# First modulation in two blocks of 512 channels, and the last FFN product in two passes of two token tiles

## The chip, the cores and the metric

The kernel runs on one core of one Trainium2 chip. The metric is the device time of one execution in microseconds (us), the median of several runs. TensorE (PE) multiplies matrices, PEld is its weight load, VectorE is DVE, ScalarE is ACT, GpSimd is POOL, and SyncE (SP) issues most of the DMAs, in order.

## The reference

Two decoder layers on 1024 tokens of 1024 channels, in float32. What matters here:

```
c_act = silu(c)
for l in range(2):
    mod = c_act @ ada_w[l] + ada_b[l]               # 6 x 1024: shift_m, scale_m, gate_m, shift_f, ...
    h = rms_norm(x, g_pre_mix[l]) * (1 + scale_m) + shift_m
    proj = h @ w_in[l] + b_in[l]                    # q (512), k, v (256), u (512)
    ...                                             # attention, pooling mixer, output projection
    x = x + gate_m * rms_norm(mix, g_post_mix[l])
    h = rms_norm(x, g_pre_ffn[l]) * (1 + scale_f) + shift_f
    f = (silu(h @ w_gate[l]) * (h @ w_up[l])) @ w_down[l]
    x = x + gate_f * rms_norm(f, g_post_ffn[l])
```

## The kernel before

The tokens are taken in two halves of 512 (T), each in four tiles of 128 (NT). Every wide product is three float32r products of high and low parts (`mm3`, L228 to L233): `split` (L208) makes the high part on ACT (L210) and the low part on DVE (L211). Each operand is loaded, split, and used by TensorE. A scheduler of the framework lays out each engine's instructions ahead of time, by program order among what its own model of the time takes to be ready; on the chip each engine and each queue then runs in that fixed order, held by semaphores.

**The start.** `xs` are the four x tiles of the first half (L1173). `load_cols` (L280) fetches the small parameter rows over SP (L287) and transposes them. The shift and scale of layer 0's first norm are made in four blocks of 256 channels: `ada_first_load` (L295) fetches, for each of the two parts, a block of `ada_w[0]` (L300); `ada_first` (L303) multiplies its eight rows j with `c_act` and adds them up on DVE (L309, L311), 256 wide, for both parts; then TensorE adds over the partitions with a product against a column of ones (L317), and DVE adds the bias (L324, L329). `pre_norm_piece(0, k, ...)` transposes 128 channels of the normalised x (L461), applies scale and shift on ACT (L466) and splits the result into an `hT` tile. `q_pass` and `kv_pass` (L613, L587) then take channels k: 12 wide products (512 columns) and 12 narrow ones (256 columns) for each k. The loop at L1190 runs over the blocks: two pieces, the next block's modulation, two steps of `q_pass`, one of `kv_pass`. The second half's x is loaded (L1198) in the third round, into the `cfa` tiles that the modulation used, and normalised (L1199) for the later stages.

**The end.** The FFN's last product, `down` (L1077), is a Strassen scheme of seven products p1 to p7, of 11 blocks of 128 rows each; the blocks come in groups (L1060) of one and then two. For each group the left operand is loaded from DRAM (L1130) and split, the right operand is combined by `combine` (L1084) in place and split into `bh` and `ph` or `bl`, and four token tiles t accumulate in four PSUM banks. The last job is p4, with the right operand `combine(b21, b21, b12)`. When a tile is done, `e7` or `e4` adds it up (L1089) and `ended` takes the square sum (ACT, L410); for p4 of the last layer it calls `finish`: a chain of 12 small DVE instructions gives 1/rms (L418, L240 to L247), then per half row `scaled_add` multiplies by 1/rms and G, the gate times `g_post_ffn` (L510) and adds x (L511), and SP stores it (L544). The four tiles of the first half are finished in the same way (`between`, L1341) while p7 and p3 run.

Of the kernel before, what the change touches and what calls it, by code (L numbers as in the profile page):

```python
# [65 lines left out]
def hybrid_decoder_kernel(  # L66
# [146 lines left out]
    def weight(*srcs):  # L213
# [9 lines left out]
        return hi, lo  # L223

    ALLP = slice(0, P)
    tiles = [slice(t * P, (t + 1) * P) for t in range(NT)]
# [53 lines left out]
    def load_cols(l):  # L280
        rows = t_("rows", [P, P])[:NROW]
        r = 0
        for src, n in (
            (ada_b[l], 6 * KD), (g_pre_mix[l], KD), (g_pre_ffn[l], KD),
            (pool_scale[l], 4), (b_in[l, QKV:INW], 4),
        ):
            nc.sync.dma_start(rows[r : r + n, :], src.rearrange("(r p) -> r p", p=P))  # L287
            r += n
        bank = msc_bank()
        nc.tensor.transpose(bank[:, :NROW], rows, ident[:NROW, :NROW])  # L290
        cols = t_("cols", [P, NROW])
        nc.vector.tensor_copy(cols, bank[:, :NROW])
        return cols

    def ada_first_load(part, n0):  # L295
        w = t_("cfa" if n0 // (2 * P) % 2 else "cfb", [P, 4, T]).rearrange("p (j a) n -> p j (a n)", j=2).rearrange("p a (j n) -> p (a j) n", n=2 * P)
        src = ada_w[0].rearrange("(p j) n -> p j n", j=KD)
        c0 = part * D + n0
        for js in (slice(0, KD // 2), slice(KD // 2, KD)):
            nc.sync.dma_start(w[:, js, :], src[:, js, c0 : c0 + 2 * P])  # L300
        return w

    def ada_first(n0, ws, cols, ab):  # L303

        accs = [t_("ar", [P, 512])[:, : 2 * P] for _ in ws]
        for j in range(KD):
            for acc, w in zip(accs, ws):
                if j == 0:
                    nc.vector.tensor_scalar(acc, w[:, j, :], c_act[:, 0:1], None, op0=ALU.mult)  # L309
                else:  # L310
                    nc.vector.scalar_tensor_tensor(  # L311
                        acc, w[:, j, :], c_act[:, j : j + 1], acc, op0=ALU.mult, op1=ALU.add
                    )
        bank = msc_bank()
        for m in range(2):
            for i in range(2):
                nc.tensor.matmul(  # L317
                    bank[:, 2 * m + i : 2 * m + i + 1], accs[m][:, i * P : (i + 1) * P], ones[:, 0:1],
                    start=True, stop=True,
                )  # L320
        o = slice(n0 // P, n0 // P + 2)
        for m, part in enumerate((1, 0)):
            k0 = part * KD + n0 // P
            nc.vector.tensor_add(ab[:, m, o], bank[:, 2 * m : 2 * m + 2], cols[:, k0 : k0 + 2])  # L324
        ada_scale(ab, 0, o, cols)
# [115 lines left out]

    def after(ins, prev):
        tc.add_manual_dep(
            ins.ins, prev.ins.name,
            mybir.DependencyInfo(mybir.DependencyClass.NoSync, mybir.DependencyReason.DATA),
            reason="order on the same engine",
        )

    def pre_norm_raw(h, k, ab, prev=None, xs=None, hf=None):
# [82 lines left out]
    def finish(h, t, fn, ss, G, xt=None):  # L532

        rstd = inv_rms(ss[:, 2 * t : 2 * t + 2])
        rows = slice(t * P, (t + 1) * P)
        for i in range(2):
            cs = slice(i * 512, (i + 1) * 512)
            if xt is None:
                x_ = t_("ar", [P, 512])
                nc.sync.dma_start(x_, spill[h][rows, cs])  # L540
            else:
                x_ = xt[:, cs]
            scaled_add(fn[t][:, cs], rstd, G[:, cs], x_)
            nc.sync.dma_start(out[0, h * T + rows.start : h * T + rows.stop, cs], fn[t][:, cs])  # L544
# [42 lines left out]
    def kv_pass(l, hT, bq, qkvs, pairs=None):  # L587

        if pairs:
            dsts = [pairs[t // 2][:, t % 2 * 256 : t % 2 * 256 + 256] for t in range(NT)]  # L590
        else:
            dsts = [acc_bank()[:, :256] for _ in range(NT)]
        for k in range(KD):
            if k % 2 == 0:
                wh, wl = weight(
                    (ALLP, 2, w_in[l, k * P : (k + 2) * P, ATT:QKV].rearrange("(a p) n -> p a n", p=P))
                )
# [12 lines left out]
        for t in range(NT):  # L610
            nc.vector.tensor_add(qkvs[t][:, ATT:QKV], dsts[t], bq[:, ATT:QKV])

    def q_pass(l, hT, bq, qkvs):  # L613
        banks = [acc_bank() for _ in range(NT)]
        for k in range(KD):
            wh, wl = weight((ALLP, None, w_in[l, k * P : (k + 1) * P, 0:ATT]))
            hi, lo = hT[k]
# [458 lines left out]

    def down(l, wd, load, kept, fn, ended):  # L1077

# [35 lines left out]
        def e4(t, bank):  # L1114
# [5 lines left out]
            ("p3", "s4", b22.__getitem__, e3), ("p7", "s3", combine(b22, b12, b11), e7),  # L1120
            ("p4", "a22", combine(b21, b21, b12), e4),
        ]
        ahead = {"p1": B21, "p2": B12, "p5": B22}
        count = [0]
        for name, a, right, evict in jobs:
            banks = [acc_bank() for _ in range(NT)]
            for g, (p0, p1) in enumerate(DOWN_GROUPS):
                n = p1 - p0
                raw = part("raw", 1024).rearrange("p (i n) -> p i n", n=512)[:, :n, :]
                nc.sync.dma_start(raw, kept[a][:, p0:p1, :])  # L1130
                lh, ll = (part(tag, 1024).rearrange("p (i n) -> p i n", n=512)[:, :n, :] for tag in ("hi", "lo"))
                split(lh, ll, raw)
                src = right(g)
# [5 lines left out]
                if name in ahead:  # L1139
                    load(ahead[name], g)  # L1140
                whole = g in (1, len(DOWN_GROUPS) - 1)
                for some in [range(n)] if whole else [(i,) for i in range(n)]:
                    for t in range(NT):
                        for i in some:
                            mm3(
                                banks[t], lh[:, i, tiles[t]], ll[:, i, tiles[t]], *rights[i],
                                p0 + i == 0, p0 + i == NPAIR - 1,
                            )
                        if p1 == NPAIR and some[-1] == n - 1:
                            evict(t, banks[t])  # L1150
                            ended(name, t)
                for _ in range(n):
# [8 lines left out]
    def layer_rows(l, d):  # L1161
        bq = t_("bqkv", [P, QKV])
        nc.sync.dma_start(bq, b_in[l : l + 1, 0:QKV].to_broadcast([P, QKV]))
        sk = t_("sk", [P, NH])
        nc.sync.dma_start(sk, sinks[l : l + 1, :].to_broadcast([P, NH]))
        nc.vector.tensor_scalar(sk, sk, -1.0, None, op0=ALU.mult)
        d["bq"], d["nsink"] = bq, sk

    par = layer_cols(0)
# [5 lines left out]
    ada0 = [ada_first_load(part, 0) for part in (1, 0)]  # L1175
    normalise(0, xs, stats(xs), True)
    hts = {0: []}
    layer_rows(0, par)
    qkvs0 = [t_("qkv", [P, QKV]) for _ in range(NT)]
    queries0 = q_pass(0, hts[0], par["bq"], qkvs0)  # L1180
# [3 lines left out]
    def first_modulation(n0):  # L1184
        if n0 < D:
            ws = [ada_first_load(part, n0) for part in (1, 0)] if n0 else ada0
            ada_first(n0, ws, par["cols"], par["abm"])
# [18 lines left out]
    for l in range(DEPTH):  # L1206
# [112 lines left out]
        def ended(name, t):  # L1319
# [29 lines left out]
        run(  # L1349
            down(l, wd, load, kept, fn, ended), 7 * NPAIR,  # L1350
            (between(), 7 * NPAIR), (side, 3 * len(jobs) * ADA),
# [40 lines left out]
```

## Time and profile before

| | us |
|---|---|
| median of 3 runs (lowest, highest) | 1993.48 (1992.32, 1997.05) |
| the profiled execution, its own time | 1994.2 |
| span of that execution, first to last instruction | 1992.4 |
| PE busy in the span | 1888.4 (95%) |
| DVE busy | 1574.2 (79%) |
| ACT busy | 957.9 (48%) |

The profile shows one execution. 1.8 us of its own time lie outside its span. A busy TensorE is not the same as a TensorE at its peak, since matmuls overlap and run at one of two clocks.

### The profile page before, as it was taken

What the parts mean: (1) busy time and instruction counts of PE and PEld (TensorE: products, weight loads), DVE (VectorE), ACT (ScalarE), POOL (GpSimd) and SP (SyncE); (2) the same over time, 40 slices, a digit from 0 to 9 for tenths busy, and PEclk for the clock granted to TensorE, in tenths of its full rate; (3) what the DMA queues carried; (4) which work ended last, traced back from release to release, by engine and by line L of the source; (5) the groups of instructions that cost most, each with busy time, mean ns of one, the idle gap of its engine ahead of it and who ended that gap; (6) DMA issues with size and microseconds to landing.
All of it is one profiled execution on the core that took longest, in us unless ns stands there. A gap on an engine that the chain in (4) does not pass through costs nothing. (4 is left out here: it accounts for less than half of the span.)

```text
span 1992.4 us, 26087 instructions
## 1 busy us (share of the span) xinstructions
PE 1888.4 (95%) x8942; PEld 1555.2 (78%) x8942; DVE 1574.2 (79%) x2951; ACT 957.9 (48%) x1797; POOL 52.8 (3%) x100
## 2 busy tenths in 40 slices
PE   4889989999999999999999899899999999999996
PEld 4777778887888887778887777788788888878885
DVE  7788976669889886786878899656888888677686
ACT  4676785563222223444757658845522222234442
POOL 1000000011000000001000000000200000000000
PEclk9999999999999999999999899999999999999998
DMA  8645654465455456842556455446555654474351
GB/s 264 206 133 156 191 177 138 131 199 194 165 184 201 147 164 219 301 140 87 185 177 188 133 151 188 132 132 193 169 182 178 199 176 148 172 256 140 114 168 64
DMA packets 224644, 340.81 MB, mean 171 GB/s; under 512 B 16728, under 2 KB 121320, under 8 KB 224512
## 3 DMA queue, kind: packets, MB, share of 16 engines
q1 hardware_dynamic: 224480, 339.15, 51.6%
q8 instruction: 70, 1.15, 0.2%
q14 instruction: 62, 0.51, 0.1%
q0 software_dynamic: 32, 0.00, 0.0%
HBM read 264.10 MB, written 74.99 MB: 170 GB/s over the span
## 5 line engine op out<-in xcount | busy, mean ns | idle before, releaser
L210 ACT ACTIVATE hi<-raw 128x1024 fp32r<-128x1024 f32 (+1 forms) x382 | 331.6, 877 | 336.6 <-PE acc L232 219.3
L211 DVE TENSOR_TENSOR lo<-raw,hi 128x1024 fp32r<-128x1024 f32 (+1 forms) x382 | 380.5, 1001 | 81.8 <-ACT hi L210 81.4
L229 PE MATMUL acc<-t,hi 128*128 128x512 f32 x704 | 275.9, 392 | 5.3 <-ACT hi L210 5.3
L233 PE MATMUL acc<-t,lo 128*128 128x512 f32 x704 | 275.5, 392 | 3.8 <-DVE lo L211 3.8
L232 PE MATMUL acc<-t,hi 128*128 128x512 f32 x704 | 275.2, 391 | 0.0
L229 PE MATMUL acc<-bh,hi 128*128 128x512 f32 x616 | 239.1, 392 | 3.3 <-ACT bh L210 3.0
L233 PE MATMUL acc<-bh,lo 128*128 128x512 f32 x616 | 241.9, 393 | 0.0
L229 PE MATMUL acc<-hT,hi 128*128 128x512 f32 x480 | 192.2, 400 | 8.7 <-ACT hi L210 8.1
L1011 DVE TENSOR_TENSOR fn<-acc,fn 128x512 f32<-128x512 f32 x220 | 151.2, 687 | 52.6 <-PE acc L233 51.9
L232 PE MATMUL acc<-hT,hi 128*128 128x512 f32 x480 | 190.6, 397 | 0.0
L233 PE MATMUL acc<-hT,lo 128*128 128x512 f32 x480 | 188.0, 395 | 0.0
L229 PEld LDWEIGHTS acc<-t,hi 128*128 128x128 f32 x704 | 133.0, 189 | 34.4 <-ACT hi L210 7.1
L233 PEld LDWEIGHTS acc<-t,lo 128*128 128x128 f32 x704 | 133.0, 189 | 34.1 <-DVE lo L211 6.6
L232 PEld LDWEIGHTS acc<-t,hi 128*128 128x128 f32 x704 | 132.9, 189 | 27.7
L232 PE MATMUL acc<-ph,hi 128*128 128x512 f32 x376 | 150.1, 399 | 0.5 <-DVE ph L211 0.4
L229 PEld LDWEIGHTS acc<-bh,hi 128*128 128x128 f32 x616 | 115.7, 188 | 31.6 <-ACT bh L210 3.8
L233 PEld LDWEIGHTS acc<-bh,lo 128*128 128x128 f32 x616 | 116.7, 189 | 24.5
L210 ACT ACTIVATE bh<-two_b 128x512 fp32r<-128x512 f32 x120 | 74.8, 623 | 98.2 <-PE acc L233 91.0
L263 DVE SCALAR_TENSOR_TENSOR ada<-ar,c_act,ada 128x512 f32<-128x512 f32 x140 | 104.8, 748 | 15.3 <-DMA ar<-in_ada_w_dram 14.0
L229 PEld LDWEIGHTS acc<-hT,hi 128*128 128x128 f32 x480 | 91.6, 191 | 28.9 <-ACT hi L210 9.6
L949 ACT ACTIVATE fn<-fn 128x512 f32<-128x512 f32 x44 | 27.8, 633 | 166.3 <-DVE fn L1011 156.1
L233 PEld LDWEIGHTS acc<-hT,lo 128*128 128x128 f32 x480 | 91.2, 190 | 18.5
(271 smaller groups left out, 3794.7 us busy)
## 6 DMA issues: line engine op xcount, KB each, us to landing
ar<-in_ada_w_dram SPq DMA_DIRECT2D x160, 256.0 KB
raw<-in_w_gate_dram SPq DMA_DIRECT2D x44, 512.0 KB
raw<-in_w_up_dram SPq DMA_DIRECT2D x44, 512.0 KB
raw<-in_w_in_dram SPq DMA_DIRECT2D x80, 256.0 KB
raw<-keeps SPq DMA_DIRECT2D x40, 512.0 KB
keeps<-fn SPq DMA_DIRECT2D x66, 256.0 KB
raw<-keepa SPq DMA_DIRECT2D x30, 512.0 KB
two_b<-in_w_down_dram SPq DMA_DIRECT2D x30, 512.0 KB
```

The costliest lines, as they stand in the source:

```text
L210: nc.scalar.activation(hi, src, AF.Copy)
L211: nc.vector.tensor_sub(lo, src, hi.bitcast(F32))
L229: ins = nc.tensor.matmul(dst, lh, rh, start=first, stop=False)
L232: nc.tensor.matmul(dst, lh, rl, start=False, stop=False)
L233: return nc.tensor.matmul(dst, ll, rh, start=False, stop=last)
L263: nc.vector.scalar_tensor_tensor(acc, w, c_act[:, i : i + 1], acc, op0=ALU.mult, op1=ALU.add)
L949: nc.scalar.activation(g, g, AF.Silu)
L1011: nc.vector.tensor_add(halves_of(dst)[m], bank, halves_of(src)[m])
```

## The change

In `load_cols` and `layer_rows` the seven small loads of layer 0 go out on ACT's queue instead of SP's. The first modulation has two blocks of 512 channels. In the first block only the scale (part 1) is added up on DVE; the shift (part 0) is added up on TensorE: each 128x128 piece of `ada_w` is the stationary operand against a column of `c_act`, and all accumulate in one PSUM bank. Its loads go into the eight `hT` tiles, two rows j at a time, scale and shift by turns. The second block works as before, 512 wide, from the `cfa` and `cfb` tiles. The order is: first loads of q and kv weights, first block, four pieces, four steps of q and two of kv (the second block's loads are issued after the first pair), second block, the second half's x, then the same again. In `down` p4's right operand is split once, into tiles that took the place of `b12` and `b22`, and its `combine` moves into p7's loop. In the last layer p4 runs over all groups for tiles 0 and 1 and then once more for tiles 2 and 3, with left operands of 256 tokens. The products with G are taken out of the last `finish`: `ended` multiplies p7's and p4's halves by G, and `finish` needs one instruction per half row.

```diff
-            nc.sync.dma_start(rows[r : r + n, :], src.rearrange("(r p) -> r p", p=P))
+            (nc.sync if l else nc.scalar).dma_start(rows[r : r + n, :], src.rearrange("(r p) -> r p", p=P))
...
+    def ada_first_load(n0):
+        src = ada_w[0].rearrange("(p j) n -> p j n", j=KD)
+        ws = []
+        step = 4 if n0 else 2
+        for j in range(0, KD, step):
+            for part in (1, 0):
+                if n0:
+                    w = t_("cfb" if j else "cfa", [P, 4, T])
+                else:
+                    w = t_("hT", [P, 2 * T]).rearrange("p (j n) -> p j n", n=T)
+                c0 = part * D + n0
+                nc.sync.dma_start(w, src[:, j : j + step, c0 : c0 + T])
+                ws.append((part, j, w))
+        return ws
...
+        accs = {part: t_("ar", [P, 512]) for part in ((1,) if pe else (1, 0))}
+        for part, j0, w in ws:
+            for j in range(w.shape[1]):
+                c_ = c_act[:, j0 + j : j0 + j + 1]
+                if pe and part == 0:
+                    for i in range(4):
+                        ins = nc.tensor.matmul(
+                            bank[:, 4 + i : 5 + i], w[:, j, i * P : (i + 1) * P], c_,
+                            start=j0 + j == 0 and i == 0, stop=False,
+                        )
...
+                acc = accs[part]
+                if j0 + j == 0:
+                    nc.vector.tensor_scalar(acc, w[:, j, :], c_, None, op0=ALU.mult)
+                else:
+                    nc.vector.scalar_tensor_tensor(acc, w[:, j, :], c_, acc, op0=ALU.mult, op1=ALU.add)
...
             if xt is None:
...
+                scaled_add(fn[t][:, cs], rstd, G[:, cs], x_)
             else:
-                x_ = xt[:, cs]
-            scaled_add(fn[t][:, cs], rstd, G[:, cs], x_)
+                nc.vector.scalar_tensor_tensor(
+                    fn[t][:, cs], fn[t][:, cs], rstd, xt[:, cs], op0=ALU.mult, op1=ALU.add
+                )
...
+                if name == "p7":
+                    right4(g)
+                products(name, g, lh, ll, rights, banks, range(NT), evict)
...
+        name, a, _, evict = jobs[-1]
+        kept4 = []
+        for ts in ((0, 1), (2, 3)) if last else (range(NT),):
+            banks = {t: acc_bank() for t in ts}
+            for g, (p0, p1) in enumerate(DOWN_GROUPS):
+                n = p1 - p0
+                lh, ll = left_of(a, p0, p1, ts[0] * P, (ts[-1] + 1) * P)
+                if len(kept4) == g:
+                    tag = "one_" if p1 == 1 else "two_"
+                    pair = [t_(tag + b, [P, n, 512], F32R) for b in (B12, B22)]
+                    split(*pair, b21[g])
+                    kept4.append([[r[:, i, :] for r in pair] for i in range(n)])
+                products(name, g, lh, ll, kept4[g], banks, ts, evict)
...
-    first_modulation(0)
-    for n0 in range(0, D, 2 * P):
-        for k in (n0 // P, n0 // P + 1):
-            hts[0].append(pre_norm_piece(0, k, par["abm"], None, xs))
-        first_modulation(n0 + 2 * P)
-        for _ in range(2):
-            next(queries0)
-        next(keys0)
-        if n0 == D - 4 * P:
+    next(queries0)
+    next(keys0)
+    ada_first(0, ada0, par["cols"], par["abm"], True)
+    for half in range(2):
+        for k in range(half * HK, (half + 1) * HK):
+            hf = t_("uT", [P, HALO + T])[:, :T]
+            hts[0].append(pre_norm_piece(0, k, par["abm"], None, xs, None, hf))
+        for pair in range(HK // 2):
+            for _ in range(2):
+                next(queries0)
+            next(keys0)
+            if half == 0 and pair == 0:
+                ada1 = ada_first_load(D // 2)
+        if half == 0:
+            ada_first(D // 2, ada1, par["cols"], par["abm"], False)
             xs1 = load_residual(1)
...
             elif name == "p7":
                 square_sum(ss[1], t, 1, fn[1][t][:, 512:D])
+                if not nxt:
+                    nc.vector.tensor_mul(fn[1][t][:, 512:D], fn[1][t][:, 512:D], G[:, 512:D])
             elif name == "p4":
                 square_sum(ss[1], t, 0, fn[1][t][:, 0:512])
                 if not nxt:
+                    nc.vector.tensor_mul(fn[1][t][:, 0:512], fn[1][t][:, 0:512], G[:, 0:512])
                     finish(1, t, fn[1], ss[1], G, tail[t])
```

## Rows read from the trace of the kernel before

**Rows 1.** The page, busy us, share of the span, instructions of TensorE
```profile
PE 1888.4 (95%) x8942; PEld 1555.2 (78%) x8942; DVE 1574.2 (79%) x2951; ACT 957.9 (48%) x1797; POOL 52.8 (3%) x100
```

**Rows 2.** The timeline of TensorE, first 75 us: start, us, operation, idle before
```profile
22.63 1.01 PE L317 MATMUL msc<-ones_r,ar 128*128 128x1 f32 x4 [0.30 <-DVE ar L311]
29.98 0.99 PE L317 MATMUL msc<-ones_r,ar 128*128 128x1 f32 x4 [6.33 <-DVE ar L311]
30.83 1.20 PE L229 MATMUL acc<-hi,hT 128*128 128x512 f32 x2
...
32.25 0.63 PE L233 MATMUL acc<-hi,hT 128*128 128x512 f32 x1
...
42.44 1.04 PE L461 MATMUL msc<-ident,fn 128*128 128x128 f32 x8
...
54.92 0.50 PE L317 MATMUL msc<-ones_r,ar 128*128 128x1 f32 x4
55.28 0.48 PE L232 MATMUL acc<-lo,hT 128*128 128x512 f32 x1
...
74.61 0.40 PE L229 MATMUL acc<-hT,hi 128*128 128x512 f32 x1
```

**Rows 3.** Windows: stretch, length, busy PE, PEld, DVE, ACT, POOL, PEclk, DMA, GB/s
```profile
42.40:45.40 3.00, 2.51 (x23) 2.19 (x21) 2.57 (x8) 2.32 (x4) 0.00 (x0) 1.00 0.03 8
45.40:53.80 8.40, 8.40 (x51) 7.46 (x49) 8.37 (x22) 3.47 (x6) 0.00 (x0) 1.00 0.37 110
...
81.00:92.00 11.00, 9.36 (x57) 7.30 (x55) 9.22 (x31) 8.80 (x17) 0.00 (x0) 1.00 0.66 190
92.00:98.00 6.00, 4.18 (x18) 3.63 (x17) 4.17 (x14) 5.38 (x14) 0.00 (x0) 0.72 0.07 26
```

**Rows 4.** The timeline of TensorE, first and last product of p4
```profile
1944.46 0.39 PE L229 MATMUL acc<-bh,hi 128*128 128x512 f32 x1
...
1975.09 0.39 PE L233 MATMUL acc<-bh,lo 128*128 128x512 f32 x1
```

**Rows 5.** The timeline of DVE, the end
```profile
1971.39 0.69 DVE L1089 TENSOR_TENSOR sa<-acc,sa 128x512 f32<-128x512 f32 x1 [8.20 <-PE acc L233]
...
1976.65 1.41 DVE L510 SCALAR_TENSOR_TENSOR sa<-sa,rs,G 128x512 f32<-128x512 f32 x2
...
1988.14 1.28 DVE L511 TENSOR_TENSOR sb<-sb,hT 128x512 f32<-128x512 f32 x2
```

**Rows 6.** The timeline of DVE where p7 ends and p4 begins
```profile
1942.20 2.48 DVE L1089 TENSOR_TENSOR sa<-acc,sa 128x512 f32<-128x512 f32 x4
...
1947.58 1.23 DVE L211 TENSOR_TENSOR lo<-raw,hi 128x1024 fp32r<-128x1024 f32 x1
```

**Rows 7.** Instructions of the line of combine, from 1780 us on
```profile
L1084 DVE TENSOR_TENSOR two_b<-two_b,two_b x10: 1217/1220/1226, 1822.6 to 1845.1; 128x1024 f32<-128x1024 f32 x10
```

**Rows 8.** Instructions by line: DVE's sums of 256 and of 512 columns: ns min/median/max
```profile
L311 DVE SCALAR_TENSOR_TENSOR ar<-cfb,c_act,ar x28: 477/481/489, 12.3 to 44.0; 128x256 f32<-128x256 f32 x28
...
L263 DVE SCALAR_TENSOR_TENSOR ada<-ar,c_act,ada x140: 740/748/755, 64.9 to 1613.4; 128x512 f32<-128x512 f32 x140
```

**Rows 9.** The DMA view of the first 60 us, GB/s in 40 slices of 1.5 us
```profile
GB/s 0 128 336 292 366 332 287 329 352 343 275 253 331 377 358 376 380 382 350 348 313 104 277 274 299 307 368 180 25 0 11 40 315 193 1 117 407 415 306 388
```

**Rows 10.** Timelines of DVE, ACT and SP, the start
```profile
11.89 0.35 DVE L309 TENSOR_SCALAR ar<-cfb,c_act 128x256 f32<-128x256 f32 x1 [0.28 <-DMA cfb<-in_ada_w_dram]
...
5.06 0.63 ACT L410 ACTIVATE junk<-fn 128x512 bf16<-128x512 f32 x1 [2.49 <-DMA fn<-in_x_dram]
...
24.13 1.45 ACT L466 ACTIVATE raw<-msc,colp 128x512 f32<-128x512 f32 x2 [1.16 <-DVE colp L329]
25.47 1.14 ACT L210 ACTIVATE hT<-raw 128x512 fp32r<-128x512 f32 x2
...
3.60 0.53 SPq L287 DMA_DIRECT2D rows<-in_ada_b_dram  x1
```

**Rows 11.** The chain that ended last, in order of time, one piece
```profile
1921.03 3.63 DMA ar<-x
```

More of the change, by code (lines that the diff above doesn't have):

```diff
@@ L223, in weight, with after @@
         return hi, lo
+    def after(ins, prev):
+        tc.add_manual_dep(
+            ins.ins, prev.ins.name,
+            mybir.DependencyInfo(mybir.DependencyClass.NoSync, mybir.DependencyReason.DATA),
+            reason="order on the same engine",
+        )
     ALLP = slice(0, P)
@@ new lines, in ada_first_load, with ada_first @@
+        ws = []
[4 more added lines that the diff above has]
+                    w = t_("cfb" if j else "cfa", [P, 4, T])
+                else:
+                    w = t_("hT", [P, 2 * T]).rearrange("p (j n) -> p j n", n=T)
[3 more added lines that the diff above has]
+        return ws
+    def ada_first(n0, ws, cols, ab, pe):
+        bank = msc_bank()
+        accs = {part: t_("ar", [P, 512]) for part in ((1,) if pe else (1, 0))}
[8 more added lines that the diff above has]
+                        )
+                        if j0 + j == 0 and i == 0:
+                            opening = ins
+                        else:
+                            after(ins, opening)
+                    continue
+                acc = accs[part]
[3 more added lines that the diff above has]
+                    nc.vector.scalar_tensor_tensor(acc, w[:, j, :], c_, acc, op0=ALU.mult, op1=ALU.add)
+        for m, part in enumerate((1,) if pe else (1, 0)):
+            for i in range(4):
+                ins = nc.tensor.matmul(
+                    bank[:, 4 * m + i : 4 * m + i + 1], accs[part][:, i * P : (i + 1) * P], ones[:, 0:1],
+                    start=not pe, stop=not pe or i == 3,
+                )
+                if pe:
+                    after(ins, opening)
+        o = slice(n0 // P, n0 // P + 4)
@@ L440, in normalise @@
         normed[h] = dst
[L442 to L447, printed above, removed]
     def pre_norm_raw(h, k, ab, prev=None, xs=None, hf=None):
@@ L592, in kv_pass, with rows @@
             dsts = [acc_bank()[:, :256] for _ in range(NT)]
+        def rows(k):
+            return weight(
+                (ALLP, 2, w_in[l, k * P : (k + 2) * P, ATT:QKV].rearrange("(a p) n -> p a n", p=P))
+            )
+        ahead = None
+        if pairs:
+            ahead = rows(0)
+            yield
         for k in range(KD):
             if k % 2 == 0:
-                wh, wl = weight(
-                    (ALLP, 2, w_in[l, k * P : (k + 2) * P, ATT:QKV].rearrange("(a p) n -> p a n", p=P))
-                )
+                (wh, wl), ahead = ahead or rows(k), None
+            elif pairs and k + 1 < KD:
+                ahead = rows(k + 1)
             cs = slice(k % 2 * 256, k % 2 * 256 + 256)
@@ L611, in kv_pass, with q_pass, rows @@
             nc.vector.tensor_add(qkvs[t][:, ATT:QKV], dsts[t], bq[:, ATT:QKV])
-    def q_pass(l, hT, bq, qkvs):
+    def q_pass(l, hT, bq, qkvs, first=False):
         banks = [acc_bank() for _ in range(NT)]
+        def rows(k):
+            return weight((ALLP, None, w_in[l, k * P : (k + 1) * P, 0:ATT]))
+        ahead = None
+        if first:
+            ahead = rows(0)
+            yield
         for k in range(KD):
-            wh, wl = weight((ALLP, None, w_in[l, k * P : (k + 1) * P, 0:ATT]))
+            wh, wl = ahead or rows(k)
+            ahead = rows(k + 1) if first and k + 1 < KD else None
             hi, lo = hT[k]
@@ L1075, in down_loads, with down @@
         return wd, load
-    def down(l, wd, load, kept, fn, ended):
+    def down(l, wd, load, kept, fn, ended, last):
         (c11, c12), (c21, c22) = [[[c[:, i * 512 : (i + 1) * 512] for c in fn[h]] for i in range(2)] for h in range(2)]
@@ L1120, in down, with left_of, products @@
             ("p3", "s4", b22.__getitem__, e3), ("p7", "s3", combine(b22, b12, b11), e7),
-            ("p4", "a22", combine(b21, b21, b12), e4),
+            ("p4", "a22", None, e4),
         ]
+        right4 = combine(b21, b21, b12)
+        def left_of(a, p0, p1, c0, c1):
+            n, w = p1 - p0, c1 - c0
+            raw, lh, ll = (
+                part(tag, 2 * w).rearrange("p (i n) -> p i n", n=w)[:, :n, :] for tag in ("raw", "hi", "lo")
+            )
+            nc.sync.dma_start(raw, kept[a][:, p0:p1, c0:c1])
+            split(lh, ll, raw)
+            return lh, ll
+        def products(name, g, lh, ll, rights, banks, ts, evict):
+            p0, p1 = DOWN_GROUPS[g]
+            n = p1 - p0
+            whole = g in (1, len(DOWN_GROUPS) - 1)
+            for some in [range(n)] if whole else [(i,) for i in range(n)]:
+                for t in ts:
+                    sl = tiles[t - ts[0]]
+                    for i in some:
+                        mm3(
+                            banks[t], lh[:, i, sl], ll[:, i, sl], *rights[i],
+                            p0 + i == 0, p0 + i == NPAIR - 1,
+                        )
+                    if p1 == NPAIR and some[-1] == n - 1:
+                        evict(t, banks[t])
+                        ended(name, t)
         ahead = {"p1": B21, "p2": B12, "p5": B22}
         count = [0]
-        for name, a, right, evict in jobs:
+        for name, a, right, evict in jobs[:-1]:
             banks = [acc_bank() for _ in range(NT)]
@@ L1128, in down @@
                 n = p1 - p0
[L1129 to L1132, printed above, removed]
+                lh, ll = left_of(a, p0, p1, 0, T)
                 src = right(g)
@@ L1140, in down @@
                     load(ahead[name], g)
[L1141 to L1151, printed above, removed]
+                if name == "p7":
+                    right4(g)
+                products(name, g, lh, ll, rights, banks, range(NT), evict)
+                for _ in range(n):
+                    yield
+        name, a, _, evict = jobs[-1]
[3 more added lines that the diff above has]
+            for g, (p0, p1) in enumerate(DOWN_GROUPS):
+                n = p1 - p0
+                lh, ll = left_of(a, p0, p1, ts[0] * P, (ts[-1] + 1) * P)
[5 more added lines that the diff above has]
+                products(name, g, lh, ll, kept4[g], banks, ts, evict)
                 for _ in range(n):
@@ L1349, in hybrid_decoder_kernel @@
         run(
-            down(l, wd, load, kept, fn, ended), 7 * NPAIR,
+            down(l, wd, load, kept, fn, ended, not nxt), 7 * NPAIR,
             (between(), 7 * NPAIR), (side, 3 * len(jobs) * ADA),
```

41 lines of the change are left out of this document (9 added, 32 removed).

## The prediction

> **What bounds the kernel now.** I read the page first: TensorE is busy for 95% of the span [rows 1], so an edit can only win where TensorE waits or where nothing is left for it. I then listed TensorE's timeline at both ends. At the start its first wide product begins at 30.83 us, and q and kv of the first half are done at 74.61, where the u products follow without a pause [rows 2]. Between the two, 8 channels k cost four stretches like that of 45.40 to 53.80, which TensorE fills [rows 3]: 4 x 8.4 = 33.6 us of products in 43.8 us. The rest is the half clock (32.25: 0.63 us for a product that later takes 0.39; the first pair needs 30.83 to 42.44, some 2.5 us more than a pair and its sums of ones) and gaps such as that of 42.40 to 45.40. At the end TensorE's last product starts at 1975.09 [rows 4] and is over some 0.4 us later, at about 1975.5; the span ends at 1992.4. These 16.9 us are DVE: from the first sum at 1971.39 to the last addition's end at about 1988.8 it hardly stops [rows 5]. So the reader should look at two places of 30 and 17 us where TensorE has nothing to do; the 1,900 us between are not touched, but for layer 0's p4.
>
> **The end, part by part.** DVE's 17.4 us for four tiles are, by start-to-start steps of 0.60 for a sum, 0.66 for L510 and 0.60 for L511 (an x2 row of 1.41 is one step and one instruction of 0.75) [rows 5, 6]: 4 x 0.60 + 8 x 0.66 + 8 x 0.60 = 12.5 us, which leaves 4.9 for four chains of 12 small instructions, 1.2 each. Afterwards only tiles 2 and 3 come late: tile 2 is done 6 products, 1.4 us, before TensorE's end T. Their work: 2 sums 1.2, 2 products with G at a sum's price 1.2, 4 fused instructions 2.6, 2 chains 2.5 to 3.5 (two chains fill each other's waits less well than four). That is 7.5 to 8.5 us from T - 1.4, so DVE ends at about T + 6.7. What follows DVE now, 1992.4 - 1988.8 = 3.6 us of stores, stays. The end moves from T + 16.9 to T + 10.3: **-6.6** (bounds -7.2 and -6.0). Tiles 0 and 1 are finished under the 15 us of the second pass: about 9 us of DVE beside 6 left splits of 0.6, which fits.
>
> T itself can move. p4 starts at 1944.46 [rows 4]; 132 products in 30.9 us are 0.23 each. Its first two groups, three blocks, now feed TensorE for 2 tiles x 3 blocks x 3 x 0.23 = 4.1 us instead of 8.2. From 1942.20 DVE works off p7's eight sums (the row shows four, four more follow), 8 x 0.60 [rows 6], and now also 4 products with G, 2.4: it is free at 1949.4, and the third group's operands cost it 0.60 (left, 512 wide, as a sum) and 1.14 (right, 1024 wide, 1.23 less the overlap): 1951.1, against 1948.6 at which TensorE asks. That is a stall of 2.5 us if the scheduler does nothing earlier, and none if it splits right operands ahead: their new tiles come free during p7. I take **+1.5** (0 to +2.6). Later groups need 1.74 us of DVE per 2.74 of TensorE. The left loads become 12 of half the size, the splits 12 on each engine for 6, which with fewer right splits adds about 0.6 us to DVE: in the second pass, where it idles. The moved combine costs nothing: the ten instructions of p6 and p4 ran at 1822 to 1845, a hundred us ahead [rows 7], and only what they read decides that. In layer 0 p4 keeps four tiles and has its buffers longer; 0, with 1 us either way.
>
> **The start, part by part.** Removed: 64 sums of 256 columns on DVE (28 as shown from cfb, 28 from cfa, 8 first ones), 0.48 each and some 0.40 from start to start, if they overlap as the sums of [rows 6] do: 25 us [rows 8]. Added: 24 of 512 columns, 0.75 each, 0.66 a step: 15.8 us. So DVE is some 9 us lighter. But the first block is now 4.19 MB instead of 2.1, and nothing starts before it is in. With x (2.1), the bias rows and small rows (0.43) the queue must carry 6.72 MB; the slices add up to 6.0 MB at 21.0 us and reach 6.72 at 23.0 [rows 9]. The first 2.6 MB had come at 10.5 and DVE saw them at 11.89 [rows 10], 1.4 later. The last shift tile is thus there at 24.4; longer rows may gain a us. TensorE's shift: 8 rows x 4 pieces, and this trace shows two records for each such product (32 for 16): 64 records. Four of them took 29.98 to 30.83 at the half clock, 0.21 each, and 54.92 to 55.28 at the full one, 0.09 [rows 2]. At 0.21 they need 13.6 us from about 14, when the first shift tile is in: done at 27.8, then 8 records for the scale, 1.7: 29.5. From such records' end to the first wide product lie DVE's additions, ACT's L466 and the split: for the first block records ended at 23.64 [rows 2], ACT began at 24.13 and was through the first piece's split at about 26.1 [rows 10]: 2.5 us. First wide product: 32.0, against 30.83. From there: 33.6 of products, 2.5 of half clock, 6 pieces' transposes at 0.5 (42.44: eight in 1.04), 16 records of the second block 1.4, and a pause at the turn of the halves, where the second block's sums go through DVE and ACT before a product can start, 2.5 less the transposes: 1.5. Sum 42.0, done at 74.0: **-0.6** (bounds: 30.5 with no pause, -3.6; 33 with a pause of 3, +2.5). The second block's 4.19 MB and its 16 sums of 0.66 lie under the first half's 20 us.
>
> The seven loads moved to ACT's queue leave SP 7 x about 0.5 us earlier [rows 10], but the DMA engines were full, so nothing is won; ACT has 2.49 us free before x comes, which they nearly fill, and the squares behind them have slack. Early q and kv weights take TensorE's wait for the first low parts away. The second half's x can load some 10 us sooner, since cfa is free sooner. Between 81 and 98 TensorE is idle for 11.00 - 9.36 + 6.00 - 4.18 = 3.5 us, behind ACT and DVE [rows 3]; a piece of that may go: **-1.0** (0 to -3).
>
> **The sum.** -6.6 + 1.5 - 0.6 - 1.0 = -6.7. The profiled execution took 1994.2, 0.7 above the median of 1993.48; on the median the forecast is 1986.8. Its own range is 1983.5 to 1990.
>
> **Rivals.** *The clock rises during the shift sums.* TensorE now has 64 records to run from 14 us on, where it had been waiting for 6.33 us before 29.98 and found the half clock at 32.25 [rows 2]. If those records bring it to 2.4 GHz, each tile takes 16 x 0.09 = 1.4 us behind its load, the last ends at 25.8, the first wide product comes at 29.0 and no half clock follows: 29.0 + 33.6 + 3.0 + 1.4 + 1.5 = 68.5, -6.1 instead of -0.6, and the time is 1981.3. Against it: they move one column each, and most of their time is weight loading. The trace has no such stretch before a rise; between 92 and 98, when TensorE was busy 4.18 of 6 us, the granted clock fell to 0.72. The Trainium skill ("TensorE: Matmul & The Clock Gate", Part 1: The HAM clock gate) says that the clock is throttled by default and that sustained activity of TensorE releases it. By that rule, if weight loads with one column behind each are activity enough, the sum is this rival's 1981.3; by the rows at hand, which show the half clock wherever TensorE had come from sparse work, it is 1986.8.
>
> *SP holds the second pass back: slower.* SP issues in order. If the four stores of tiles 0 and 1 stand ahead of left loads of the second pass, those wait for DVE's 9 us, then 3.6 us from issue to use, as the x loads for the first half's finish showed [rows 11], and 1.2 for the split: 13.8 against 4.1 us of covered work. T slips by up to 9.7 us and the time is 1996.5. It decides above a slip of 6.7. Against it: eight half-size buffers let the loads run several groups ahead.
>
> *The start loses what the end wins.* With the first wide product at 33, the shift tiles late and a full pause, the start is +2.5, the relief at 81 to 98 stays out, p4's stall is 2.6: -1.5, 1992.
>
> **Chances.** Forecast 0.53, clock 0.27, start loses 0.13, SP 0.07. The range 1980.5 to 1992 leaves out SP's case and the edges. A measurement tells about 0.3%, 6 us, from no change: below 1987.5 is faster. That takes 0.58 of the forecast's case and nearly all of the clock's: 0.56. Slower than 1999.5 needs SP's case with a late start: 0.05. The same: 0.39.
>
> **What would show it.** In the profile after: DVE's last instruction about 6.7 us behind TensorE's last; p4's sums of tiles 0 and 1 in its middle; a gap of TensorE near p4's third group, or none; 64 records of the shift before the first wide product, 0.21 or 0.09 apart; that product near 32; the u products near 74. The forecast is wrong if the first block's data come after 26 us, if the pause at the turn exceeds 3 us, or if DVE orders p4's splits behind the finishing of tiles 0 and 1.

## The result, and the profile after

The changed kernel takes 2000.63 us (median of 12 runs, 1993.77 to 2006.55) against 1992.77 (12 runs, 1990.20 to 1997.05): ratio 1.0034, 95% interval 1.0021 to 1.0048, and 1.0052 (1.0034 to 1.0069) when it was timed again. The forecast was 1986.8 with a range up to 1992: wrong in its sign. The profiled execution took 1998.92 us, its span is 1997.1. The page's row of engines, which answers to [rows 1]:

```profile
PE 1905.0 (95%) x8998; PEld 1564.7 (78%) x8998; DVE 1565.4 (78%) x2901; ACT 955.8 (48%) x1793; POOL 49.0 (2%) x100
```

56 records more and 16.6 us more of busy TensorE: 64 records of shift products at 0.215 are 13.8. The timeline of TensorE over the first 77 us (answers to [rows 2]), and two of the issues on ACT's queue:

```profile
16.05 0.35 PE L297 MATMUL msc<-ident,rows 72*128 72x72 f32 x1 [16.05 <-DMA rows<-in_b_in_dram]
16.20 6.94 PE L328 MATMUL msc<-c_act,hT 128*128 128x1 f32 x32
23.00 1.95 PE L483 MATMUL msc<-ident,fn 128*128 128x128 f32 x8
24.74 6.83 PE L328 MATMUL msc<-c_act,hT 128*128 128x1 f32 x32
31.43 1.85 PE L344 MATMUL msc<-ones_r,ar 128*128 128x1 f32 x8
33.69 2.02 PE L483 MATMUL msc<-ident,fn 128*128 128x128 f32 x8 [0.41 <-DVE colp L358]
36.15 0.79 PE L236 MATMUL acc<-hi,hT 128*128 128x512 f32 x1 [0.44 <-ACT hT L210]
...
39.57 0.39 PE L240 MATMUL acc<-hi,hT 128*128 128x512 f32 x1
...
76.56 0.39 PE L236 MATMUL acc<-hT,hi 128*128 128x512 f32 x1
...
10.91 0.34 ACTq L294 DMA_DIRECT2D rows<-in_ada_b_dram  x1
...
12.56 0.31 ACTq L294 DMA_DIRECT2D rows<-in_b_in_dram  x1
```

The first wide product comes at 36.15 (forecast 32.0, before 30.83). Up to 31.4 TensorE works without a break from 16.05 on, and it starts late: the small transpose L297 heads its queue and waits for parameter rows that ACT issued only between 10.91 and 12.56, behind six of its squares. The 64 records are 0.215 apart, the price that the prediction read from records at the half clock; products of 0.63 end at about 39.3. The u products begin at 76.56, not at 74.0.

The end, timelines of TensorE and DVE (answers to [rows 4] and [rows 5]):

```profile
1956.74 0.50 PE L236 MATMUL acc<-one_b,hi 128*128 128x512 f32 x1 [0.35 <-DVE sa L1136]
...
1986.17 0.39 PE L240 MATMUL acc<-two_b,lo 128*128 128x512 f32 x1
...
1970.50 0.69 DVE L1136 TENSOR_TENSOR sa<-acc,sa 128x512 f32<-128x512 f32 x1 [2.35 <-PE acc L240]
...
1978.71 1.41 DVE L568 SCALAR_TENSOR_TENSOR sa<-sa,rs,hT 128x512 f32<-128x512 f32 x2
...
1986.60 0.69 DVE L1136 TENSOR_TENSOR sb<-acc,sb 128x512 f32<-128x512 f32 x1 [0.67 <-PE acc L240]
...
1992.59 1.41 DVE L568 SCALAR_TENSOR_TENSOR sb<-sb,rs,hT 128x512 f32<-128x512 f32 x2
```

Tiles 0 and 1 are finished in the middle of p4, at 1980. TensorE ends at T = 1986.56, the span at 1997.15: T + 10.6, forecast T + 10.3. The one stall of TensorE in p4's first pass is 0.35.

So the end gave its 6.4 us, the start lost 2 to 3, and yet the execution is 4.7 us longer. The rest was lost where nothing had been changed. I matched each DVE and ACT instruction of the two traces by its name and count, and took how far the one of after lies behind the one of before (median in stretches of 80 us that begin at the time given; the kernels of the other columns come below):

```
us of before  after  after_again  after_aligned  before_off384  end_only  shift_dve
   80           2.3      2.2          1.3           -2.4         -3.0      -3.6
  400           5.7      5.3          0.5           -1.0         -1.4      -2.9
  800           6.9      8.3          2.6            0.3         -0.8      -3.2
 1200           6.4     10.1          1.4           -0.1         -2.5      -5.8
 1600          10.4     13.2          2.3            3.2         -2.3      -5.9
 1760          11.1     13.8          2.4            3.9         -2.3      -5.9
```

After loses 9 us between 80 and 1760. From 90 us on the instructions of every engine stand in the same order in both kernels there, but for those of layer 0's down; ahead of 90 us 16 u products of TensorE and a few instructions of DVE and ACT stand elsewhere. TensorE's waits between 78 and 1950 us are 62.1 us in after and 58.1 in before, so more than half of the 9 us is no wait: the same products took longer. (The profile of before had itself lost some 3 us by 100 us, about half of it to a granted clock of 0.91 between 80 and 100: the columns of end_only and before_off384, with the same start and a granted clock of 1.00 there, show it.)

### The profile page after: what moved, and what is told of

It is laid out like the page before. It is cut to its first block, busy times and chain, and to the rows that moved or that the text cites. A ratio compares the mean times of both kernels' runs of the same rounds, so it can differ in the third digit from the quotient of the medians.

```text
span 1997.1 us, 26131 instructions
## 1 busy us (share of the span) xinstructions
PE 1905.0 (95%) x8998; PEld 1564.7 (78%) x8998; DVE 1565.4 (78%) x2901; ACT 955.8 (48%) x1793; POOL 49.0 (2%) x100
## 5 line engine op out<-in xcount | busy, mean ns | idle before, releaser
L236 PE MATMUL acc<-bh,hi 128*128 128x512 f32 x528 | 203.8, 391 | 3.0 <-ACT bh L210 3.0
L240 PE MATMUL acc<-bh,lo 128*128 128x512 f32 x528 | 206.2, 390 | 0.0
L236 PE MATMUL acc<-hT,hi 128*128 128x512 f32 x480 | 193.6, 403 | 10.3 <-ACT hi L210 9.7
L239 PE MATMUL acc<-ph,hi 128*128 128x512 f32 x320 | 127.8, 399 | 0.5 <-DVE ph L211 0.4
L236 PEld LDWEIGHTS acc<-bh,hi 128*128 128x128 f32 x528 | 98.8, 187 | 26.5 <-ACT bh L210 3.8
L236 PEld LDWEIGHTS acc<-hT,hi 128*128 128x128 f32 x480 | 91.3, 190 | 32.1 <-ACT hi L210 11.2
L240 PEld LDWEIGHTS acc<-bh,lo 128*128 128x128 f32 x528 | 99.7, 189 | 21.0
L239 PEld LDWEIGHTS acc<-hT,hi 128*128 128x128 f32 x480 | 91.3, 190 | 19.2 <-issue 0.2
```

The source lines that it names most:

```text
L236: ins = nc.tensor.matmul(dst, lh, rh, start=first, stop=False)
L239: nc.tensor.matmul(dst, lh, rl, start=False, stop=False)
L240: return nc.tensor.matmul(dst, ll, rh, start=False, stop=last)
```

## The experiments

**Which part.** Two kernels split the change, one moves the transpose that TensorE's queue waited for, one repeats after. Theory A: the new start costs the middle; B: chance; C: the new p4 of layer 0.

```diff
 # rows_late, against after: load_cols(0) only loads; ada_first transposes behind its products
-        bank = msc_bank()
-        nc.tensor.transpose(bank[:, :NROW], rows, ident[:NROW, :NROW])
+        def turn():
+            bank = msc_bank()
+            nc.tensor.transpose(bank[:, :NROW], rows, ident[:NROW, :NROW])
...
+        cols = cols() if callable(cols) else cols
```

end_only. 

> The kernel before with the edits of down, finish and ended alone; the first modulation as before. Theory A (the 9 us that the stretch from 140 to 1840 us loses in the trace of after come with the edits of the start, which leave the order of the instructions there as it was but shift which buffers and moments they meet): the tail gains its 6.4 us, p4's first pass costs some 0.4, so about 1986.7, ratio 0.997, and the profile lies within 2 us of before's at 1840 us. Theory B (those 9 us are chance between two executions): the same 1986.7 here. Theory C (the new p4 of layer 0 and its buffers cost the middle): ratio 1.000 to 1.003, and the profile loses 5 us or more behind 880 us.

start_only. 

> The kernel before with the edits of the start alone; down, finish and ended as before. Theory A (the start's edits cost the middle): 2 us at the start and 9 or more behind it: 2003 to 2007, ratio 1.005 to 1.007. Theory B (chance): 2 us at the start alone, 1994.8, ratio 1.001. Theory C (the end's edits cost the middle): 1994.8 too, with a profile that keeps its 2 us up to 1840 us.

rows_late. 

> The changed kernel, but the transpose of layer 0's small parameter rows is issued behind the first eight shift products instead of ahead of them. In after that transpose waited for its rows until 16.05 us with the shift products queued behind it, while the first scale tile had been on hand at 12.76. The first shift products should start at 13.3 to 14 and the first wide product come 2.2 to 2.8 us earlier, near 33.7, if TensorE's 64 records set it; if the loads set it, under 0.5 us earlier. In time: theory A without more, about 1998 (after minus 2.4); if the loss of the middle hangs on the moment at which the middle is entered, it may move by several us either way, and its profile's lag will show that.

after_again. 

> The changed kernel once more, as a control. Theory A: 2000 to 2001, and its second profile again loses some 9 us against before between 140 and 1840 us, in the same stages (up projections of both layers). Theory B (chance): the losses fall elsewhere or stay out in this profile, though the median of many runs stays near 2000.

Measured: end_only 1986.01 us (0.9963, 0.9951 to 0.9976), start_only 2007.49 (1.0081, 1.0062 to 1.0100), after_again 2004.04, beside 1992.49 for before. The end alone does what was forecast; the start alone costs 15 us, and the second trace of after drifts like the first. B and C fall, A stands, but its reason (the moments at which instructions meet their buffers) is not enough, as rows_late shows: its first shift products start at 14.03 and its first wide product at 34.91, 1.2 us earlier than after (2.2 to 2.8 were expected), and yet it takes 2009.13 (1.0079, 1.0054 to 1.0103). Between 480 and 700 us, where after's wide products follow each other by 0.2268 us, much as before's do (0.2269), those of rows_late take 0.2289, for 200 us on end. Nothing there differs but where the tiles lie.

**The place of an operand in SBUF**, the memory on the chip in which the tiles lie. A shared tag, the name under which a set of buffers is reused, gets its place at its first use. Before, `cols`, `colp`, `rs`, `junk` and `sk` came early, and hT began at byte 59904, 117 times 512. After, `ada_first_load` uses hT first, and it begins at byte 37248, which is 384 past a multiple of 512; raw, hi and lo stay on multiples. In rows_late `cols` moves too, and hi and lo are 448 past one. Theory D: a wide product steps slower when an operand starts off such a place. Edits that use tags early without doing anything test it with every instruction and every order unchanged (fn and the small tags move with hT, so the step is read below by operand):

```diff
 # after_aligned, against after (aligned_late: the same on rows_late, with t_("st"...), t_("ss"...) too)
+    t_("cols", [P, NROW])
+    t_("colp", [P, 2, KD])
+    t_("rs", [P, 8])
+    t_("junk", [P, 512], BF16)
+    t_("sk", [P, NH])
     xs = []
...
 # before_off384, against before (off256, off448, off128: some of the small tags ahead of hT)
+    t_("hT", [P, 2 * T])
+    t_("cols", [P, NROW])
...
```

after_aligned. 

> The changed kernel with no instruction changed and none reordered: five small tags (cols, colp, rs, junk, sk; 2176 bytes) get their places in SBUF ahead of fn and hT instead of behind them, so that hT begins at a multiple of 512 bytes, as in the kernel before, and not 384 bytes past one. Theory D (a wide product steps slower when an operand does not begin at a multiple of 512 bytes): in the traces the step of such products is 0.233 us where hT moves and 0.232 where hT is stationary, against 0.227; 1440 x 6.3 ns + 384 x 5.3 ns = 11 us come back, so 1988 to 1993, and in the profile the products with hT between 400 and 460 us step 0.227 again. Rival E (the drift comes from the moments at which buffers and loads meet, set going by the new start): nothing that a place changes, 2000 to 2004.

before_off384. 

> The kernel before with no instruction changed and none reordered: hT gets its place first and so begins 384 bytes past a multiple of 512, as in after; the five small tags follow, so that raw, hi and lo stay at multiples of 512. Theory D: 11 us slower than before, about 2003.5, ratio 1.0055, and the products with hT step 0.232 to 0.234. Rival E: no change, 1992.5.

before_off256. 

> The same with hT 256 bytes past a multiple of 512. Theory D with 256 bytes as the unit: no change, 1992.5, steps of 0.227. Theory D with 512 as the unit: slower by 4 to 11 us, 1996 to 2003.5, steps of hT's products between 0.229 and 0.234. Rival E: no change.

aligned_late. 

> The changed kernel with the transpose of the parameter rows behind the first eight shift products, as in rows_late, and with all tags placed so that fn, hT, raw, hi, lo, ada and ph begin at multiples of 512 bytes (ph, 384 past one even in the kernel before, by placing ss ahead of ada). Theory D: before's 1992.5, less 6.1 at the end, plus 1.3 at the start (2.0 less the 0.7 of its slow products), less 2.2 for the transpose, less 320 products with ph x 6.6 ns = 2.1: about 1983.5, and faster than end_only. Rival E: like rows_late, 2000 or more.

before_off448. 

> The kernel before with hT 448 bytes past a multiple of 512 (a multiple of 64, not of 128), one profile for the step of its products. Theory D with 256 bytes as the unit and the same price for every other place: 0.233 where hT moves, 0.232 where it is stationary. If the price depends on how far off it is: rows_late, with hi and lo 448 past as stationary operands, had 0.2292, and both operands 448 past 0.2271, so less than 0.233 is likely.

before_off128. 

> The same with hT 128 bytes past a multiple of 512. Theory D with 256 bytes as the unit: as at 384, 0.233 where hT moves, 0.232 where it is stationary. If only some places cost: 0.227.

Measured: after_aligned 1995.46 us (1.0014, 1.0001 to 1.0026; 1988 to 1993 by theory D), before_off384 1998.49 (1.0028, 1.0017 to 1.0040; 2003.5 by D), before_off256 1993.02 (1.0002, 0.9993 to 1.0011), aligned_late 1994.45 (1.0001, 0.9990 to 1.0013), beside 1992.9. One profile each of before_off448 and before_off128 took 1998.52 and 1999.64. The view of instructions by line and shape between 405 and 440 us, the second product of `mm3` with hT moving, in before, before_off128, before_off256, before_off384 and before_off448 (the mean ns stand behind the busy time):

```profile
L232 PE MATMUL acc<-hT,hi 128*128 128x512 f32 x49 | 19.1, 390 | 0.0
```

```profile
L232 PE MATMUL acc<-hT,hi 128*128 128x512 f32 x47 | 18.5, 395 | 0.0
```

```profile
L232 PE MATMUL acc<-hT,hi 128*128 128x512 f32 x48 | 18.7, 389 | 0.0
```

```profile
L232 PE MATMUL acc<-hT,hi 128*128 128x512 f32 x47 | 18.5, 394 | 0.0
```

```profile
L232 PE MATMUL acc<-hT,hi 128*128 128x512 f32 x47 | 18.6, 396 | 0.0
```

Five or six ns a product come and go with the place alone. The starts of the products show it in another way; TensorE in after, 16 products one behind the other, and in after_aligned, 18:

```profile
420.07 0.39 PE L236 MATMUL acc<-hT,hi 128*128 128x512 f32 x1
420.30 0.39 PE L239 MATMUL acc<-hT,hi 128*128 128x512 f32 x1
420.53 0.39 PE L240 MATMUL acc<-hT,lo 128*128 128x512 f32 x1
...
423.55 0.39 PE L236 MATMUL acc<-hT,hi 128*128 128x512 f32 x1
```

```profile
413.07 0.39 PE L236 MATMUL acc<-hT,hi 128*128 128x512 f32 x1
413.30 0.39 PE L239 MATMUL acc<-hT,hi 128*128 128x512 f32 x1
413.52 0.39 PE L240 MATMUL acc<-hT,lo 128*128 128x512 f32 x1
...
416.92 0.39 PE L240 MATMUL acc<-hT,lo 128*128 128x512 f32 x1
```

3.48 / 15 = 0.2320 and 3.85 / 17 = 0.2265. Over whole traces, each product matched to its operands in the program, the mean step from a product with hT to the next one with hT in the same role (steps under 0.26 us) in before and the four kernels with hT moved is:

```
start of hT, bytes past a multiple of 512      0       128     256     384     448
hT moving (1302 to 1314 steps each)          0.2275  0.2325  0.2275  0.2325  0.2333
hT stationary (304 to 318 each)              0.2287  0.2323  0.2285  0.2322  0.2294
```

A start 256 past costs nothing. Theory D, with 256 bytes as the unit, holds for the step, and E, which wanted no change, falls. D's price for the time was too high: the step grows by 5.0 and 3.5 ns here, not by 6.3 and 5.3, and not in every product. Matched one by one with before from 78 us on, the products of before_off384 whose step stays under 0.3 us in both profiles are 6.5 us longer with hT moving (1341 of 1440) and 0.7 us with hT stationary (247 of 384); those that ran beside a wait or at the half clock show nothing clear. All of TensorE is 5.5 us longer there, and the kernel took 5.6 us more. For after, the place is 5.2 to 8.6 us (1995.46 against 2000.63 and 2004.04); the same match of after with after_aligned gives 6.7 and 0.8. aligned_late, forecast at 1983.5, shows that the place is not all: with no operand of a wide product off a multiple of 256 but a few, it is only level with before.

**The shift sums on TensorE.** After_aligned is still 9.4 us behind end_only, which differs by the start alone, and its runs spread from 1990 to 2000 where those of end_only spread over 3 us. One literal moves the first block's shift sums to DVE; look_a and look_b are two further profiles of after_aligned, for the spread; end_ph places ph well too, which no kernel had done.

```diff
 # shift_dve, against after_aligned
-    ada_first(0, ada0, par["cols"], par["abm"], True)
+    ada_first(0, ada0, par["cols"], par["abm"], False)
...
 # end_ph, against end_only; shift_dve_ph, against shift_dve: ahead of the loop over xs
+    t_("st", [P, 8])
+    t_("ss", [P, 8])
```

shift_dve. 

> after_aligned with the first block's shift summed on DVE too (24 wide sums of the start become 32), so that TensorE has no shift products ahead of its first wide product. Theory F (the start's loss is TensorE's 64 records at the half clock, 13.8 us from 15.9 us on, in front of the transposes): the last sum is done some 1 us behind the last tile of data, near 27, eight products with ones follow, and the first wide product comes near 32.5 instead of 35.8: 3 us less, 1992.5. Rival G (the loads set it: 4.19 MB must be in before anything starts): under 1 us less, 1994.5 to 1995.5.

look_a. 

> after_aligned once more, one profile: its times spread from 1990 to 2000 while those of end_only, with the start of before, spread from 1984 to 1987. If this execution is a late one, its profile shows where: in stretches at the half clock (the mean granted clock of late executions was 0.979 to 0.984, that of early ones 0.985 to 0.986) if the clock makes the spread, or in waits for loads if the DMA queues make it.

look_b. 

> after_aligned again, a second single profile, for the same question as look_a: where a late execution loses its time, in stretches at the half clock or in waits for loads.

end_ph. 

> The kernel before with the end's edits alone (as end_only), and ss placed ahead of ada so that ada and ph begin at multiples of 512 bytes; no other instruction or order changed. Theory D: ph is the moving operand of 320 wide products in the down stages, 6.6 ns each, and TensorE is never idle there: 2.1 us under end_only's 1986.0, so 1983.9, with steps of 0.2267 instead of 0.228 from 880 to 970 and 1780 to 1950 us. Rival: the 2 us come back as waits, 1986.0.

shift_dve_ph. 

> shift_dve with ss placed ahead of ada, so that ada and ph begin at multiples of 512 bytes too: the end's edits, the start with both sums on DVE, and every tag of the wide products placed well. If the gains add up: end_ph took 4.1 us off end_only, so 1982.8 - 4.1 = 1978.7; by products with ph alone (320 x 6.6 ns) 1980.7. If the new start with sums on DVE is worth nothing against the old one: as end_ph, 1982.

Measured: shift_dve 1982.83 us (0.9950, 0.9935 to 0.9965), end_ph 1981.91 (0.9942, 0.9930 to 0.9954), shift_dve_ph 1981.21 (0.9942, 0.9930 to 0.9954), beside 1992.71 (1992.37 for the last); look_a and look_b 2000.63 and 1997.72. Placing ph well took 4.1 us off end_only, where 2.1 had been worked out, and 1.6 off shift_dve; in end_ph the products of the down stages step 0.2267 instead of 0.228. TensorE in shift_dve:

```profile
26.02 1.87 PE L344 MATMUL msc<-ones_r,ar 128*128 128x1 f32 x8 [9.72 <-DVE ar L341]
27.75 1.95 PE L483 MATMUL msc<-ident,fn 128*128 128x128 f32 x8
29.48 1.71 PE L344 MATMUL msc<-ones_r,ar 128*128 128x1 f32 x8
31.60 2.02 PE L483 MATMUL msc<-ident,fn 128*128 128x128 f32 x8 [0.41 <-DVE colp L358]
33.70 0.80 PE L236 MATMUL acc<-hi,hT 128*128 128x512 f32 x1
...
72.76 0.40 PE L236 MATMUL acc<-hT,hi 128*128 128x512 f32 x1
...
91.04 0.80 PE L236 MATMUL acc<-hT,hi 128*128 128x512 f32 x1 [2.51 <-ACT hi L210]
```

The sums end on DVE at 28.5, and the first wide product comes 2.1 us before after_aligned's 35.81 (3.3 were forecast), the u products at 72.76 against 75.96. G, the loads as the bound, falls; F's mechanism stands, but the gain is 12.6 us, not 3. The other part is what follows. In shift_dve the scheduler laid the attention's beginning in another order, in which TensorE waits once up to 100 us, for 2.5 us; in after_aligned, as in before, it waits four times:

```profile
87.69 0.36 PE L775 MATMUL msc<-sa,qT 128*128 128x256 f32 x1 [2.31 <-ACT qT L765]
90.97 0.36 PE L775 MATMUL msc<-sa,qT 128*128 128x256 f32 x1 [0.58 <-ACT qT L765]
92.06 0.50 PE L236 MATMUL acc<-hT,hi 128*128 128x512 f32 x1 [0.38 <-ACT hi L210]
96.89 0.50 PE L236 MATMUL acc<-hT,hi 128*128 128x512 f32 x1 [1.80 <-ACT hi L210]
```

That is 5.1 us. In before the first of the four was 0.67 (first line, before; second, after):

```profile
85.03 0.36 PE L728 MATMUL msc<-sa,qT 128*128 128x256 f32 x1 [0.67 <-ACT qT L718]
88.46 0.36 PE L775 MATMUL msc<-sa,qT 128*128 128x256 f32 x1 [2.30 <-ACT qT L765]
```

In before seven u products, 1.6 us, stood between the transposes and this product and covered the wait; in after, after_aligned and start_only they run ahead of the transposes. In look_a the same waits are followed by the half clock, in after_aligned they are not. Windows, after_aligned and then look_a (the granted clock, PEclk, stands behind the engines):

```profile
85.00:90.00 5.00, 2.69 (x23) 2.37 (x22) 3.25 (x9) 3.93 (x8) 0.00 (x0) 1.00 0.56 183
90.00:95.00 5.00, 4.03 (x20) 2.86 (x18) 3.57 (x13) 4.97 (x12) 0.00 (x0) 1.00 0.60 176
100.00:105.00 5.00, 5.00 (x38) 4.58 (x37) 2.61 (x11) 4.36 (x13) 0.00 (x0) 1.00 0.52 156
```

```profile
85.00:90.00 5.00, 2.70 (x21) 2.58 (x20) 2.34 (x8) 3.06 (x6) 0.00 (x0) 0.85 0.54 165
90.00:95.00 5.00, 4.32 (x24) 3.69 (x24) 4.14 (x15) 4.50 (x7) 0.00 (x0) 0.81 0.48 142
100.00:105.00 5.00, 5.00 (x33) 4.68 (x32) 3.48 (x11) 3.14 (x6) 0.00 (x0) 0.79 0.11 33
```

By 120 us look_a lies 3.6 us behind after_aligned. But shift_dve's profile has the half clock behind its wait too (granted clock 0.66 from 90 to 95 us), so such a stretch alone does not make an execution late. From 123 us on the order is the same in all of them, and yet the distance to shift_dve at 1760 us is 8.3 us for after_aligned (the profile of its fastest execution), 18.4 for look_a, 15.8 for look_b. After_aligned's 8.3 are accounted for: 3.2 at the u products and 5.5 of longer waits (58.3 against 52.8 us from 78 to 1760 us). In look_a and look_b, 3.9 and 9.0, or 4.1 and 7.7, leave 5.5 and 4.0 that are no waits. The half clock explains little of that: from 78 to 1950 us it was granted for 54.6 us in shift_dve and for 58.0 in each of the two, at most 1.7 us (half of the 3.4) of lost work more. Why a later start makes later waits longer, and what else is lost in some executions, stays open.

## Why the prediction was wrong

**The step that failed** is the sentence "the 1,900 us between are not touched, but for layer 0's p4". At the u products the start had lost 2.0 us (76.56 against 74.61); all the rest was lost in that stretch, for two reasons. The first is the place. But for the down stages no instruction behind 90 us was changed or reordered there, yet hT lay elsewhere, and products with it stepped 0.232 to 0.233 instead of 0.227: 5.2 to 8.6 us. The trace of before could have warned, in its view of TensorE by line and shape:

```profile
L232 PE MATMUL acc<-ph,hi 128*128 128x512 f32 x376 | 150.1, 399 | 0.5 <-DVE ph L211 0.4
L232 PE MATMUL acc<-bl,hi 128*128 128x512 f32 x240 | 94.0, 392 | 0.0
```

The same line's products took 399 ns with ph and 392 with bl, and ph was 384 bytes off there. The second reason is the start.

**The start, -0.6,** was missed in its size and in what it set going: with hT in its place the new start costs 9.4 us (1995.5 against 1986.0). Costed right: 64 records of 0.215, no rise of the clock during them. Costed wrong: the shift products began at 16.2, not at 14, because the loads moved to ACT's queue were held to be free while TensorE's first transpose depended on them; one run of eight transposes, 1.7 us, stood between the shift products. The upper bound was also added up wrongly: 33 with a pause of 3 gives 76.5, +1.9 and not +2.5, and 76.56 is just at it. Not costed: the longer wait at the attention's beginning, and the longer waits and late executions behind it. The chain of kernels that differ by one part each gives the prices: before 1992.5, with the end 1986.0 (-6.5), with the new start but all sums on DVE and hT in its place 1982.8 (-3.2), with the shift on TensorE 1995.5 (+12.6), with hT off its place 2000.6 to 2004.0 (+5.2 to +8.6). So the blocks of 512 were right and the TensorE sum was what hurt, though the 12.6 include the order that the scheduler chose for either, and a part of them is not explained. Once ph lies well too, the new start (1981.21) and the old (1981.91) can't be told apart: the gains did not add up.

**The end, -6.6,** was right: -6.5 for end_only, T + 10.6 in after. Its split was partly luck. The last addition in before ends at 1989.4 (1988.14 and 1.28 in [rows 5]), not at 1988.8, so 3.0 us of stores follow DVE and not 3.6; in after DVE ends at T + 7.4, not T + 6.7, and 3.1 follow. The two errors cancel. The stall in p4's first pass, +1.5, was 0.35, at its first product: DVE got to the splits in time. Layer 0's p4, 0 with 1 us either way, changed next to nothing: TensorE in after lay 6.7 us behind before at 960 us, ahead of p4, and 6.5 at 1010 us, behind it; in end_only it was 1.3 and 1.4 ahead.

**The relief between 81 and 98 us, -1.0,** went the other way: TensorE was idle for 5.0 us there instead of 3.5 (17.00 less 11.96; before 17.00 less 13.55), which is the wait that grew from 0.67 to 2.30.

**The rivals.** The clock did not rise: the records ran 0.215 apart throughout, 14 us of them, and the first wide products behind still took 0.79 and 0.63. That rival leaned on a rule of the Trainium skill ("TensorE: Matmul & The Clock Gate", Part 1: The HAM clock gate): activity of TensorE releases its clock. By that rule, used as the rival used it, the time would have been 1981.3; the trace does not bear that use out. SP did not hold the second pass back (0.35 of stall). The start did lose, by more than its rival allowed, since that rival stopped at the u products.

## What to carry to other kernels

Before a stretch is called untouched, look where its operands lie: an edit that uses one tag earlier than another moves all tags behind it, and a TensorE-bound kernel pays for it in most of the products that read it. Compare the mean ns of one line's products by operand name in the profile; a group that is 5 to 8 ns dearer than its twin points to the place, and moving ph took 4.1 us off end_only, 2.1 of which its step explains. And cost a move onto TensorE's queue by what stands behind it in order, not by its own records alone.

## What the runs showed of the hardware

Wide float32r products stepped 0.227 us when both operands began at a multiple of 256 bytes of SBUF (0 and 256 past a multiple of 512 were run), and 0.2325 to 0.2333 when the moving one began 128, 384 or 448 past it (0.2294 to 0.2323 for the stationary one). With both operands 448 past, as for hi and lo in rows_late, the mean was 0.2282 (median 0.227), against 0.2293 for the products there whose stationary operand alone was 448 past; no run explains why. Float32 products with one moving column ran 0.215 us a record, 14 us of them, and the wide products behind them still took 0.63.
